# Attention behind a recurrent trunk: six PSUM banks for the projections, rotary tables in the first SwiGLU, rotation ahead of the norm

## The chip, the cores, the metric

The kernel is one program on one core of one Trainium2 chip. The metric is the device time of one execution, in microseconds (us), as the median of several executions. Its engines are TensorE (PE in the rows; PEld is its weight load), VectorE (DVE), ScalarE (ACT), GpSimd (POOL) and SyncE (SP). Each runs its own instructions in the order in which the program lists them and waits on the others through semaphores.

## The reference

A two-layer trunk over 512 tokens of 1024 features: a recurrent layer, a SwiGLU, then one attention layer with a shared K/V, and a second SwiGLU. The change lies in the attention, whose projections are normed per head and rotated:

```python
kv = (hn @ w_kv).reshape(B, S, N_GROUPS, 2, KV_HEADS, HEAD_DIM)   # 3 groups, 2 heads, 128
k = rms_norm(k, k_norm[:, None, :])
k = apply_partial_rope(k, cos, sin)      # first 32 of 128 features: x1*c - x2*s, x2*c + x1*s
...
q = (hn @ w_q)...                        # 3 groups x 2 kv heads x 4 query heads
q = rope(rms_norm(q, q_norm)); s = q @ k.T * HEAD_DIM ** -0.5
# softmax over a band: three dilation groups (windows 128, 512, 2048; dilations 1, 4, 16)
h = h + attention(...) @ w_o
h = h + (silu(h @ w_g) * (h @ w_u)) @ w_out
```

The norm is `y * rsqrt(mean(y*y) + eps) * gain`. Rows of the norm are single numbers per token and head, so the factor `rsqrt(...)` commutes with the rotation, which mixes features of one token and head only; the gain does not, since it differs from feature to feature.

## The kernel before, in words

The activations lie transposed, as eight tiles of 128 features x 512 tokens. Every fp32 product is made of three matmuls on high and low halves (`mm3`, L146 to L148; in the projections L676 to L678). Weights come through a class `Stream`: SP loads a 128x1024 piece (`wr`), ACT casts its high half (`wh`, L100), DVE subtracts the low one (`wl`, L107; for the query and output weights a DMA on POOL's queue adds it up). These steps have high priority; all else is ordered by a scheduler that works through the program once, so what stands in each engine's queue, and in which order, is fixed before the run.

PSUM has eight banks: four tagged "mm", two "PT" (transposes), one "S" (scores) and one "O" (values, row statistics). A tag's banks are handed out in turn, and a matmul that starts a new tile waits until all readers of the tile that had the bank before are done.

- **First SwiGLU** (`swiglu`, from L459). `norm_factors` sums squares (L240) and takes an inverse root on DVE (`rsqrt`, L205 to L215: eleven ops on 128x4, shift, subtract, and three Newton steps of three); DVE makes a diagonal `dg` (L252), a matmul spreads it over the rows (L255). Then per hidden block: `g` and `u` (L480, L482) on DVE, Silu on ACT, `u*g` on POOL (L483).
- **K/V projections** (`project`, L664). Three groups of four token tiles; each of four steps kk takes one weight piece and runs six matmuls on each of four tiles. A tile is ready after its fourth step and goes to `done_kv` (L699): `collect` copies the K half out of PSUM (L613, on ACT for K, on DVE for Q), squares it in place (L614) and sums it (L615); the V half is scaled and split by ACT (L713) and DVE (L714), in one piece per head for group 0, in two of 64 partitions per head for group 1. When the fourth tile is there, `normed` (L618) makes the inverse root (`factors`, L625 and `rsqrt`), then per tile `rotate`: one `scalar_tensor_tensor` per head for factor and gain (L635), and four ops of rotation (L642 to L645). `turn` transposes the result by PE (L730, L754). `at` and `tick` delay these calls by so many tile steps.
- **Rotary tables**. At the head of `attention`, ACT's queue issues four small loads (`far`, `grow`, `pos`, `inv`), and some 34 DVE ops on 128x128 (L542 to L582) with two Sin on ACT make `cc` and `ss`. They fall beside the first K/V projections.
- **Queries and attention**. The query projections of kv head 0 run like K/V. Those of kv head 1, and the first half of the output projection, are interleaved with attention units (`attend`, plan at the end of `attention`): per unit a `scores` call (nine matmuls into the bank S, L146 to L148; DVE's two fused reductions L804 and L807 into the negated maximum `mn`, Exp on ACT, L813, L814), three units later `turned` (transposes L829, split by ACT L223 into `ph` and DVE L224 into `pl`), and four units later `values`.

Of the kernel before, what the change touches and what calls it, by code (L numbers as in the profile page):

```python
# [139 lines left out]
def trunk(tc, A, out):  # L140
# [33 lines left out]
    with tc.tile_pool(name="keep", bufs=1) as kp, tc.tile_pool(name="wts", bufs=3) as wp, \  # L174
# [30 lines left out]
        def rsqrt(v, pool, tag):  # L205
            w = v.shape[-1]
            y = pool.tile([128, w], F32, name=tag + "y", tag=tag + "y")
            a = pool.tile([128, w], F32, name=tag + "a", tag=tag + "a")
            V.tensor_scalar(y.bitcast(I32), v.bitcast(I32), 1, None, ALU.arith_shift_right)
            V.tensor_scalar(y.bitcast(I32), y.bitcast(I32), -1.0, float(0x5F3759DF), ALU.mult, ALU.add)  # L210
            for _ in range(3):
                V.tensor_mul(a, y, v)
                V.scalar_tensor_tensor(a, a, -0.5, y, ALU.mult, ALU.mult)
                V.scalar_tensor_tensor(y, a, 1.5, y, ALU.add, ALU.mult)
            return y  # L215

# [17 lines left out]
        def gain(c, k):  # L234
            return par[:, c + k:c + k + 1]
# [250 lines left out]

        with tc.tile_pool(name="ffn1", bufs=2) as fp:
            fp = Pool(fp)

            def after_f1(m):  # L490
                split(h[m], gain(C_KV, m), xh[m], xl[m])
                squares(m, fp)

            swiglu(fp, p_f1, after_f1)


        with tc.tile_pool(name="att", bufs=2) as ap:
            ap = Pool(ap)
            attention(tc, A, ap, ws, dict(locals()))

# [15 lines left out]

def attention(tc, A, ap, ws, env):
    nc = tc.nc
    V, S, G, PE = nc.vector, nc.scalar, nc.gpsimd, nc.tensor
    h, xh, xl, ident, ssum = env["h"], env["xh"], env["xl"], env["ident"], env["ssum"]  # L520
    bank, mm3, split, halve, rsqrt = env["bank"], env["mm3"], env["split"], env["halve"], env["rsqrt"]
    gain, p_kv, p_q, p_o = env["gain"], env["p_kv"], env["p_q"], env["p_o"]

    far = ap.tile([128, 4, 160], BF16, name="far", bufs=1)
    S.dma_start(far, A["far"])
    grow = ap.tile([128, 6, 128], F32, name="grow", bufs=1)
# [4 lines left out]
    pos = ap.tile([128, 8], I32, name="pos", bufs=1)  # L531
    S.dma_start(pos, A["pos"])
    inv = ap.tile([128, 16], F32, name="inv", bufs=1)
    S.dma_start(inv, A["inv_freq"])
    posf = ap.tile([128, 8], F32, name="posf", bufs=1)
    V.tensor_copy(posf, pos)
    cc = ap.tile([128, 8, 16], F32, name="cc", bufs=1)
    ss = ap.tile([128, 8, 2, 16], F32, name="ss", bufs=1)

    tmp = [ap.tile([128, 512], F32, name="rtmp", tag="pr", bufs=N_PR) for _ in range(2)]  # L540
    ang, a1, a0, s1, k2, t = (tmp[i % 2][:, 128 * (i // 2):128 * (i // 2) + 128] for i in range(6))
# [75 lines left out]

    def normed(st, nh, tab, g_row, E, turn, lag, tiles=range(4)):  # L618
# [11 lines left out]
        def rotate(t):  # L630
            dst, r = kn[t], st["r"]
# [5 lines left out]
            x = dst.rearrange("q (h d) -> q h d", d=128)[:, :nh]  # L637
            a = ap.tile([128, 4, 32], F32, name="ra", tag="ra")[:, :nh]
            b = ap.tile([128, 4, 32], F32, name="rbt", tag="rbt", bufs=1)[:, :nh]
            cct = cc[:, tab + t].unsqueeze(1).unsqueeze(1).to_broadcast([128, nh, 2, 16])  # L640
            sst = [ss[:, tab + t, c, :].unsqueeze(1).to_broadcast([128, nh, 16]) for c in range(2)]
            E.tensor_tensor(*(v.rearrange("q h (c f) -> q h c f", c=2) for v in (a, x[:, :, 0:32])), cct, ALU.mult)  # L642
            E.tensor_tensor(b[:, :, 0:16], x[:, :, 16:32], sst[0], ALU.mult)
            E.tensor_tensor(b[:, :, 16:32], x[:, :, 0:16], sst[1], ALU.mult)
            E.tensor_tensor(x[:, :, 0:32], a, b, ALU.add)  # L645

        at(1, factors)
        for j, t in enumerate(tiles):
            at(2 + j, lambda t=t: rotate(t))
            at(lag + j, lambda t=t: turn(t, kn[t]))  # L650
# [47 lines left out]
    for g in range(3):  # L698
        def done_kv(t, ps, g=g, st={}):  # L699
            tab = 0 if g == 0 else 4  # L700
            c = slice(128 * t, 128 * t + 128)
            vv = ps[:, 256:512].rearrange("q (a d) -> q a d", a=2)
            collect(ps, 2, t, 4, st, S.copy)
            ro = rstd[0][:, tab + t:tab + t + 1]
# [20 lines left out]
            if t == 3:  # L725
# [18 lines left out]
    def project_q(kv):  # L744
        for g in range(3):

            for j, tiles in enumerate((range(2), range(2, 4)) if kv and g == 2 else (range(4),)):
                def done_q(t, ps, g=g, st={}, tiles=tiles):
                    collect(ps, 4, t - tiles[0], len(tiles), st, V.tensor_copy)
                    if t == tiles[-1]:  # L750
# [32 lines left out]
    def scores(kv, n, p):  # L783
# [39 lines left out]
    def turned(kv, n, p):  # L823
# [174 lines left out]
```

## Time and profile before

| | us |
|---|---|
| median of 3 executions | 1232.18 (1232.13 to 1233.57) |
| the profiled execution | 1235.38 |
| its span in the trace | 1233.6 |
| PE busy / DVE / ACT / POOL | 1212.2 / 686.5 / 514.8 / 113.7 |

The profile is of one execution. Its own time stands 1.8 us above the span (what lies before and after) and 3.2 us above the median. PE is busy 98% of the span, so what can be won lies in the 21.4 us in which it is not, and in stretches in which its granted clock is not full. A row of the timeline gives the start, the duration, the engine, the line, and in brackets how long the engine stood idle before it and on which instruction it waited.

### The profile page before, as it was taken

Reading aid. Unit: us, or ns where it says so; the run is one execution under the profiler, and the core shown is the slowest. Engines: PE = TensorE matmul, PEld = TensorE weight load, DVE = VectorE, ACT = ScalarE, POOL = GpSimd, SP = SyncE. Lnnn points to the kernel's source line nnn. Section 1 sums busy time; section 2 is a strip of 40 time slices with the busy share of each in tenths; the row PEclk is TensorE's granted clock in tenths of the full one; section 3 lists DMA queues with packets and bytes.
Section 4 is the critical chain, followed back from the end, with each engine's and each line's share of the span. In section 5 each row is a group of like instructions: output and inputs, shape, how many; then the busy total and the mean of one; then the engine's idle time right before and its main releaser. Section 6 shows DMA issues by size and latency. Waiting matters only on the chain.

```text
span 1233.6 us, 14762 instructions
## 1 busy us (share of the span) xinstructions
PE 1212.2 (98%) x5629; PEld 998.7 (81%) x5629; DVE 686.5 (56%) x1382; ACT 514.8 (42%) x771; POOL 113.7 (9%) x128
## 2 busy tenths in 40 slices
PE   9999999999999999998999999899999999999998
PEld 6778888888888888877888888798888888888887
DVE  7877654455454333387567677875645545443221
ACT  5795432323222222265555666665423323222110
POOL 0100001011111000010411010000001111100000
PEclk9999999999999999999999998999999999999999
DMA  6544323323323333332988665435232232333331
GB/s 224 141 116 120 103 86 103 103 88 100 99 89 99 97 104 98 102 96 85 210 183 186 137 143 132 103 69 120 86 103 88 101 96 92 103 99 103 117 116 45
DMA packets 40902, 138.15 MB, mean 112 GB/s; under 512 B 5120, under 2 KB 5760, under 8 KB 40832
## 3 DMA queue, kind: packets, MB, share of 16 engines
q1 hardware_dynamic: 32688, 111.74, 28.6%
q0 software_dynamic: 6848, 24.12, 11.4%
q10 hardware_dynamic: 1296, 1.36, 0.4%
q8 instruction: 44, 0.72, 0.2%
q14 instruction: 26, 0.21, 0.1%
HBM read 134.05 MB, written 2.10 MB: 110 GB/s over the span
## 4 chain that ended last, share of the span: by engine, by line
PE 92%; DVE 3%; ACT 3%; DMA 1%; issue 0%; ACTq 0%
PE ps L147 25%; PE ps L146 25%; PE ps L148 25%; PE ps L676 4%; PE ps L677 4%; PE ps L678 4%; PE ps L754 1%; ACT wh L100 1%; PE ps L829 1%; PE ps L382 1%; DVE kn L635 1%; DMA wr<-in_w_in 1%; PE ps L383 0%; ACT qh L223 0%; ACT wl L103 0%
## 5 line engine op out<-in xcount | busy, mean ns | idle before, releaser
L100 ACT CAST wh<-wr 128x1024 fp32r<-128x1024 f32 (+3 forms) x212 | 215.4, 1016 | 499.9 <-PE ps L147 448.4
L146 PE MATMUL ps<-xh,wh 128*128 128x512 f32 x896 | 355.2, 397 | 1.2 <-ACT xh L218 1.2
L147 PE MATMUL ps<-xl,wh 128*128 128x512 f32 x896 | 349.5, 390 | 0.3 <-DVE xl L219 0.3
L148 PE MATMUL ps<-xh,wl 128*128 128x512 f32 x896 | 349.8, 390 | 0.0
L107 DVE TENSOR_TENSOR wl<-wr,wh 128x1024 fp32r<-128x1024 f32 (+2 forms) x168 | 241.5, 1438 | 153.8 <-ACT wh L100 153.7
L146 PEld LDWEIGHTS ps<-xh,wh 128*128 128x128 f32 x896 | 168.7, 188 | 39.4 <-ACT xh L218 2.6
L147 PEld LDWEIGHTS ps<-xl,wh 128*128 128x128 f32 x896 | 168.6, 188 | 37.7 <-issue 2.6
L148 PEld LDWEIGHTS ps<-xh,wl 128*128 128x128 f32 x896 | 168.5, 188 | 35.4 <-DMA wl<-in_w_in 0.2
L146 PE MATMUL ps<-gh,wh 128*128 128x512 f32 x352 | 136.9, 389 | 0.0
L147 PE MATMUL ps<-gl,wh 128*128 128x512 f32 x352 | 136.9, 389 | 0.0
L148 PE MATMUL ps<-gh,wl 128*128 128x512 f32 x352 | 136.9, 389 | 0.0
L482 DVE TENSOR_TENSOR u<-ps,rb 128x512 f32<-128x512 f32 x44 | 30.4, 691 | 139.2 <-PE ps L148 139.2
L483 POOL TENSOR_TENSOR u<-u,g 128x512 f32<-128x512 f32 x44 | 58.0, 1318 | 497.9 <-ACT wh L100 364.5
L676 PE MATMUL ps<-wh,xh 128*128 128x512 f32 x224 | 92.1, 411 | 0.1
L678 PE MATMUL ps<-wh,xl 128*128 128x512 f32 x224 | 88.6, 395 | 0.0
L677 PE MATMUL ps<-wl,xh 128*128 128x512 f32 x224 | 88.4, 395 | 0.0
L148 PEld LDWEIGHTS ps<-gh,wl 128*128 128x128 f32 x352 | 66.1, 188 | 13.8
L146 PEld LDWEIGHTS ps<-gh,wh 128*128 128x128 f32 x352 | 66.1, 188 | 13.7
L147 PEld LDWEIGHTS ps<-gl,wh 128*128 128x128 f32 x352 | 66.1, 188 | 13.6
L480 DVE TENSOR_TENSOR g<-ps,rb 128x512 f32<-128x512 f32 x44 | 30.4, 691 | 64.5 <-PE ps L148 64.4
L103 ACT ACTIVATE wl<-wr 128x1024 fp32r<-128x1024 f32 x44 | 46.6, 1058 | 26.6 <-PE ps L677 25.6
L223 ACT CAST gh<-u 128x512 fp32r<-128x512 f32 x44 | 27.3, 621 | 59.9 <-POOL u L483 59.9
(202 smaller groups left out, 1457.4 us busy)
## 6 DMA issues: line engine op xcount, KB each, us to landing
wr<-in_f_in SPq DMA_DIRECT2D x88, 512.0 KB, 3.5
wr<-in_f_out SPq DMA_DIRECT2D x32, 512.0 KB, 3.6
wr<-in_w_q SPq DMA_DIRECT2D x28, 512.0 KB, 6.6
wl<-in_w_q POOLq DMA_DIRECT2D x28, 512.0 KB, 7.1
wr<-in_w_in SPq DMA_DIRECT2D x14, 512.0 KB, 3.9
wr<-in_f_out SPq DMA_DIRECT2D x16, 384.0 KB, 3.1
wr<-in_w_kv SPq DMA_DIRECT2D x12, 512.0 KB, 3.4
wl<-in_w_in POOLq DMA_DIRECT2D x8, 512.0 KB, 6.5
```

The costliest lines, as they stand in the source:

```text
L100: nc.scalar.copy(hi[:, c], r[:, c])
L103: nc.scalar.mul(lo[:, c], r[:, c], -1.0)
L107: a = eng.tensor_tensor(lo[:, c], r[:, c], hi[:, c].bitcast(F32), ALU.subtract)
L146: PE.matmul(ps, wh, xh, start=first, stop=False)
L147: PE.matmul(ps, wh, xl, start=False, stop=False)
L148: PE.matmul(ps, wl, xh, start=False, stop=last)
L480: V.tensor_tensor(g, pair[0], rb, ALU.mult)
L482: V.tensor_tensor(u, pair[1], rb, ALU.mult)
L483: G.tensor_tensor(u, u, g, ALU.mult)
L676: PE.matmul(ps[t], xh[k][:, r], wh[:, c], start=k == 0, stop=False)
L677: PE.matmul(ps[t], xh[k][:, r], wl[:, c], start=False, stop=False)
L678: PE.matmul(ps[t], xl[k][:, r], wh[:, c], start=False, stop=k == 7)
```

## The change

Six edits, all around the attention:

1. `project` takes its banks from a list: four "mm", then "S", then "O", four times over, which covers the 12 K/V tiles and the 12 query tiles of kv head 0; after that "mm" alone.
2. The loads and the ops of the rotary tables move out of `attention` into a function `rotary`, called in the first SwiGLU's program at its first output block, with the tables in a pool of their own.
3. `collect` multiplies by the gain while it takes the tile out of PSUM, on DVE for K and Q alike (ACT's copy of K goes).
4. The rotation is done per tile one step after `collect`, before the norm's factor is known; the factor is then one `tensor_tensor` per tile (`scale`) with a broadcast factor.
5. `rsqrt` has eight ops in place of eleven: one op for the start value, one Newton step of three and one step of higher order of four.
6. The softmax of a score and the split of its transposed rows get high priority in the scheduler.

```diff
-            V.tensor_scalar(y.bitcast(I32), v.bitcast(I32), 1, None, ALU.arith_shift_right)
-            V.tensor_scalar(y.bitcast(I32), y.bitcast(I32), -1.0, float(0x5F3759DF), ALU.mult, ALU.add)
-            for _ in range(3):
-                V.tensor_mul(a, y, v)
-                V.scalar_tensor_tensor(a, a, -0.5, y, ALU.mult, ALU.mult)
-                V.scalar_tensor_tensor(y, a, 1.5, y, ALU.add, ALU.mult)
+            V.tensor_scalar(y.bitcast(I32), v.bitcast(I32), -0.5, float(0x5F3759DF), ALU.mult, ALU.add)
+
+            s = 0.375
+            V.tensor_mul(a, y, v)
+            V.scalar_tensor_tensor(a, a, -0.5 * s, y, ALU.mult, ALU.mult)
+            V.scalar_tensor_tensor(y, a, 1.5 * s, y, ALU.add, ALU.mult)
+            V.scalar_tensor_tensor(a, y, -1.0 / (s * s), v, ALU.mult, ALU.mult)
+            V.tensor_mul(a, a, y)
+            V.scalar_tensor_tensor(a, a, 10.0 / 3.0, a, ALU.add, ALU.mult)
+            V.scalar_tensor_tensor(y, a, 5.0, y, ALU.add, ALU.mult)
...
+                def after_f1(m):
+                    split(h[m], gain(C_KV, m), xh[m], xl[m])
+                    squares(m, fp)
+                    if m == 0:
+                        tables.extend(rotary(tc, A, rp, fp))
...
-    def collect(raw, nh, j, n, st, copy):
+    def collect(raw, nh, j, n, st, tab, g_row):
...
-        copy(dst[:, :128 * nh], rows)
+        x = dst.rearrange("q (h d) -> q h d", d=128)[:, :nh]
+        V.tensor_tensor(x, rows.rearrange("q (h d) -> q h d", d=128),
+                        grow[:, g_row].unsqueeze(1).to_broadcast([128, nh, 128]), ALU.mult)
...
+        at(1, lambda: rotate(x, nh, tab))
...
-            for i in range(nh):
-                c = slice(128 * i, 128 * i + 128)
-                j = nh * (t - first) + i
-                V.scalar_tensor_tensor(dst[:, c], dst[:, c], r[:, j:j + 1], grow[:, g_row, :],
-                                       ALU.mult, ALU.mult)
...
+        def scale(t):
+            j = nh * (t - first)
+            x = kn[t].rearrange("q (h d) -> q h d", d=128)[:, :nh]
+            V.tensor_tensor(x, x, st["r"][:, j:j + nh].unsqueeze(2).to_broadcast([128, nh, 128]), ALU.mult)
...
+    free = itertools.chain(["mm", "mm", "mm", "mm", "S", "O"] * 4, itertools.repeat("mm"))
...
-                    ps[t] = bank()
+                    ps[t] = bank(next(free))
...
+    @first
+    def softmax(n, p, ps, pr, mn, g0, w, nb):
...
-        halve(pt.rearrange("q (b k) -> q b k", k=128)[:, :nb], ph[:, :nb, p % 2], pl[:, :nb, p % 2])
+        first(halve)(pt.rearrange("q (b k) -> q b k", k=128)[:, :nb], ph[:, :nb, p % 2], pl[:, :nb, p % 2])
```

How this moves instructions, at three places on DVE. In the rows a name stands for a tile (buffer numbers left in where they tell pieces apart); the lines of the changed kernel are its own.

DVE at the front of the first SwiGLU, where `nrv` to `nry` are the inverse root for the row factors and `dg` its diagonal, before:

```order
L214 SCALAR_TENSOR_TENSOR nry<-nra,nry 128x4
L212 TENSOR_TENSOR nra<-nry,nrv 128x4
L213 SCALAR_TENSOR_TENSOR nra<-nra,nry 128x4
L214 SCALAR_TENSOR_TENSOR nry<-nra,nry 128x4
L252 TENSOR_SCALAR dg<-ident,nry 128x128 x4
L107 TENSOR_TENSOR wl_1479<-wr_1445,wh_1478 128x1024
L480 TENSOR_TENSOR g<-ps,rb 128x512
```

and in the changed kernel:

```order
L217 SCALAR_TENSOR_TENSOR nra<-nra 128x4
L536 TENSOR_SCALAR grow<-grow 128x384
L218 SCALAR_TENSOR_TENSOR nry<-nra,nry 128x4
L544 CAST posf<-pos 128x8
L256 TENSOR_SCALAR dg<-ident,nry 128x128 x4
L550 TENSOR_TENSOR rtmp<-posf,inv 128x128
L555 TENSOR_SCALAR rtmp<-rtmp 128x128
```

The scheduler brought the tables' ops from the first output block to the very front: the op on `grow`, which waits for a load, now stands ahead of the last step of the inverse root and of `dg`; ten rows of the tables (some grouping several ops) follow before the next `wl`, and the rest stands behind it, up to the second `u`.

DVE in the K/V projections, where the first tiles of group 0 come out of PSUM, before (`rtmp`, `cc`, `ss` are the tables):

```order
L615 TENSOR_REDUCE sqc<-ps 128x2
L574 SCALAR_TENSOR_TENSOR rtmp<-rtmp 128x128
L714 SCALAR_TENSOR_TENSOR vl_3708<-ps,msy,vh_3706 128x128
L575 TENSOR_SCALAR rtmp<-rtmp 128x128
L714 SCALAR_TENSOR_TENSOR vl_3708<-ps,msy,vh_3706 128x128
L579 TENSOR_TENSOR rtmp<-rtmp 128x128
L578 TENSOR_TENSOR rtmp<-rtmp 128x128
L582 TENSOR_SCALAR cc<-rtmp 128x128
L581 TENSOR_SCALAR ss<-rtmp 128x8x16 x2
L714 SCALAR_TENSOR_TENSOR vl_3709<-ps,msy,vh_3707 128x128 x2
```

and in the changed kernel:

```order
L633 TENSOR_TENSOR kn<-ps,grow 128x256
L737 SCALAR_TENSOR_TENSOR vl_3707<-ps,msy,vh_3705 128x128
L648 TENSOR_TENSOR kn<-ra,rbt 128x2x32
L645 TENSOR_TENSOR ra<-kn,cc 128x64
L636 TENSOR_REDUCE sqc<-ps 128x2
L737 SCALAR_TENSOR_TENSOR vl_3708<-ps,msy,vh_3706 128x128
L646 TENSOR_TENSOR rbt<-kn,ss 128x2x16
L647 TENSOR_TENSOR rbt<-kn,ss 128x2x16
```

The tables are gone from between the V pieces; the gain's product and the rotation of the tile before stand there instead.

DVE in the attention stage, where the last two-tile block of queries of kv head 1 is normed, before (`qr4y` is the factor, `pl` and `pr` belong to attention units):

```order
L213 SCALAR_TENSOR_TENSOR qr4a<-qr4a,qr4y 128x8
L214 SCALAR_TENSOR_TENSOR qr4y<-qr4a,qr4y 128x8
L635 SCALAR_TENSOR_TENSOR kn<-kn,qr4y,grow 128x128 x5
L642 TENSOR_TENSOR ra<-kn,cc 128x128
L643 TENSOR_TENSOR rbt<-kn,ss 128x4x16
L644 TENSOR_TENSOR rbt<-kn,ss 128x4x16
L635 SCALAR_TENSOR_TENSOR kn<-kn,qr4y,grow 128x128
L645 TENSOR_TENSOR kn<-ra,rbt 128x4x32
L635 SCALAR_TENSOR_TENSOR kn<-kn,qr4y,grow 128x128 x2
```

and in the changed kernel:

```order
L217 SCALAR_TENSOR_TENSOR qr4a<-qr4a 128x8
L218 SCALAR_TENSOR_TENSOR qr4y<-qr4a,qr4y 128x8
L665 TENSOR_TENSOR kn<-kn,qr4y 128x512
L228 TENSOR_TENSOR pl<-ps,ph 128x4x128
L665 TENSOR_TENSOR kn<-kn,qr4y 128x512
L842 ISA pr,mn<-ps,ssum 128x256
L842 ISA mn 128x1
L845 ISA pr,mn<-ps,far,mn 128x256
```

From the factor to the first tile that can be transposed stood five scalings, three ops of rotation, a sixth scaling and the rotation's sum; now one `scale`. The two reductions of a softmax (L842, L845) stand side by side, where three ops of rotation stood between them before.

## Rows read from the trace of the kernel before

**Rows 1.** The page: busy time of each engine over the span.

```profile
PE 1212.2 (98%) x5629; PEld 998.7 (81%) x5629; DVE 686.5 (56%) x1382; ACT 514.8 (42%) x771; POOL 113.7 (9%) x128
```

**Rows 2.** Windows by stage: start and end, length, then busy time and (instructions) of PE, PEld, DVE, ACT and POOL, the granted clock as a share, the DMA share, GB/s. 525 to 602 holds the K/V projections, 602 to 698 the queries of kv head 0, 698 to 802 attention beside the queries of kv head 1.

```profile
525.00:545.00 20.00, 18.00 (x88) 14.88 (x87) 17.39 (x62) 14.69 (x32) 2.95 (x4) 1.00 0.36 110
...
570.00:602.00 32.00, 31.75 (x135) 25.67 (x136) 19.73 (x84) 17.15 (x37) 8.87 (x14) 0.95 0.55 134
602.00:698.00 96.00, 96.00 (x470) 79.77 (x469) 61.02 (x226) 53.98 (x81) 17.43 (x22) 1.00 0.83 180
698.00:720.00 22.00, 21.53 (x129) 18.19 (x128) 14.60 (x62) 12.42 (x23) 2.19 (x3) 1.00 0.52 120
720.00:802.00 82.00, 74.17 (x461) 64.45 (x460) 67.55 (x245) 55.20 (x105) 8.20 (x10) 0.94 0.56 129
```

**Rows 3.** PE's waits over the whole span: the line that waited, for what, total us, times, longest.

```profile
PE ps L676 <- DVE vl L714: 5.2, 2, 3.2
PE ps L146 <- DVE mn L807: 3.5, 4, 1.9
PE ps L146 <- ACT ph L223: 2.1, 2, 1.7
PE ps L754 <- DVE kn L645: 2.1, 2, 1.6
```

**Rows 4.** Timeline of PE in the K/V projections: matmuls before, and after, a wait.

```profile
543.91 0.47 PE L676 MATMUL ps<-wh,xp 128*128 128x512 f32 x1 [2.00 <-DVE vl L714]
...
549.00 0.39 PE L676 MATMUL ps<-wh,xp 128*128 128x512 f32 x1
549.22 0.39 PE L677 MATMUL ps<-wl,xp 128*128 128x512 f32 x1
...
570.16 0.47 PE L676 MATMUL ps<-wh,xp 128*128 128x512 f32 x1 [3.21 <-DVE vl L714]
570.46 0.58 PE L677 MATMUL ps<-wl,xp 128*128 128x512 f32 x1
...
573.83 0.46 PE L676 MATMUL ps<-wh,xp 128*128 128x512 f32 x1
```

**Rows 5.** Timeline of DVE and ACT in the K/V projections, where the first tiles of groups 0 and 1 come out of PSUM.

```profile
543.14 0.36 DVE L581 TENSOR_SCALAR ss<-rtmp 128x128 f32<-128x128 f32 x2
543.42 0.60 DVE L714 SCALAR_TENSOR_TENSOR vl<-ps,msy,vh 128x128 fp32r<-128x128 f32 x2
...
562.89 0.37 ACT L613 COPY kn<-ps 128x256 f32<-128x256 f32 x1 [0.39 <-PE ps L678]
...
568.40 1.23 DVE L107 TENSOR_TENSOR wl<-wr,wh 128x1024 fp32r<-128x1024 f32 x1 [0.52 <-ACT wh L100]
...
569.66 1.00 DVE L714 SCALAR_TENSOR_TENSOR vl<-ps,msy,vh 64x128 fp32r<-64x128 f32 x3
```

**Rows 6.** Timeline of DVE in the attention stage: a softmax's reductions among rotation ops, and a norm's scaling and rotation.

```profile
738.36 0.42 DVE L804 CUSTOM_DVE_ANT_0 pr<-ps,ssum 128x256 f32<-128x256 f32 x1
738.70 0.29 DVE L642 TENSOR_TENSOR ra<-kn,cc 128x128 f32<-128x128 f32 x1
739.18 0.48 DVE L807 CUSTOM_DVE_ANT_1 pr<-ps,far,mn 128x256 f32<-128x256 f32 x1
...
757.99 0.17 DVE L214 SCALAR_TENSOR_TENSOR qr4y<-qr4a,qr4y 128x8 f32<-128x8 f32 x1
758.19 1.40 DVE L635 SCALAR_TENSOR_TENSOR kn<-kn,qr4y,grow 128x128 f32<-128x128 f32 x5
...
760.25 0.28 DVE L645 TENSOR_TENSOR kn<-ra,rbt 128x128 f32<-128x128 f32 x1
```

**Rows 7.** DVE's groups of instructions between 698 and 802 us: count, busy time and mean ns of one, idle time ahead of them and its releaser.

```profile
L635 DVE SCALAR_TENSOR_TENSOR kn<-kn,qr4y,grow 128x128 f32<-128x128 f32 x48 | 14.2, 346 | 0.1
L804 DVE CUSTOM_DVE_ANT_0 pr<-ps,ssum 128x256 f32<-128x256 f32 (+1 forms) x20 | 7.7, 384 | 1.5 <-PE ps L148 1.3
L613 DVE COPY kn<-ps 128x512 f32<-128x512 f32 x8 | 5.5, 683 | 3.4 <-PE ps L678 3.4
```

**Rows 8.** The page's groups over the span: a product out of PSUM on DVE (columns as in rows 7).

```profile
L482 DVE TENSOR_TENSOR u<-ps,rb 128x512 f32<-128x512 f32 x44 | 30.4, 691 | 139.2 <-PE ps L148 139.2
```

**Rows 9.** Timeline of DVE, PE and POOL at the front of the first SwiGLU.

```profile
160.16 0.69 DVE L232 TENSOR_TENSOR ssum<-ssum,sq 128x512 f32<-128x512 f32 x1
...
167.08 0.88 DVE L252 TENSOR_SCALAR dg<-ident,nry 128x128 f32<-128x128 f32 x4
...
169.08 1.02 PE L255 MATMUL ps<-dg,ones 128*128 128x512 f32 x2
...
176.48 1.22 DVE L107 TENSOR_TENSOR wl<-wr,wh 128x1024 fp32r<-128x1024 f32 x1 [0.17 <-ACT wh L100]
...
181.06 0.69 DVE L482 TENSOR_TENSOR u<-ps,rb 128x512 f32<-128x512 f32 x1 [3.35 <-PE ps L148]
181.90 1.29 POOL L483 TENSOR_TENSOR u<-u,g 128x512 f32<-128x512 f32 x1 [7.68 <-DVE u L482]
181.96 2.30 DVE L107 TENSOR_TENSOR wl<-wr,wh 128x1024 fp32r<-128x1024 f32 x1 [0.21 <-ACT wh L100]
```

**Rows 10.** DVE's groups of instructions between 525 and 545 us (columns as in rows 7): the commonest op of the rotary tables.

```profile
L551 DVE SCALAR_TENSOR_TENSOR rtmp<-rtmp 128x128 f32<-128x128 f32 x13 | 3.7, 287 | 0.1
```

**Rows 11.** DMA issues between 518 and 540 us: what is loaded, the queue, KB, us from issue to landing.

```profile
grow<-in_row_gains ACTq DMA_DIRECT2D x1, 384.0 KB, 6.5
```

More of the change, by code (lines that the diff above doesn't have):

```diff
@@ L485, in swiglu @@
             out_proj(p[1], HB, 8, gh, gl, after)
[L487 to L499, printed above, removed]
+        with tc.tile_pool(name="tables", bufs=1) as rp:
+            rp = Pool(rp)
+            with tc.tile_pool(name="ffn1", bufs=2) as fp:
+                fp = Pool(fp)
+                tables = []
+                def after_f1(m):
[3 more added lines that the diff above has]
+                        tables.extend(rotary(tc, A, rp, fp))
+                swiglu(fp, p_f1, after_f1)
+            with tc.tile_pool(name="att", bufs=2) as ap:
+                ap = Pool(ap)
+                attention(tc, A, ap, ws, dict(locals()))
         with tc.tile_pool(name="ffn2", bufs=2) as fp:
@@ L514, with rotary @@
 START_Q = 11
-def attention(tc, A, ap, ws, env):
+def rotary(tc, A, rp, tp):
     nc = tc.nc
[L519 to L524, printed above, removed]
+    V, S = nc.vector, nc.scalar
+    rp.tile([128, 16], F32, name="pad")
+    far = rp.tile([128, 4, 160], BF16, name="far", bufs=1)
     S.dma_start(far, A["far"])
-    grow = ap.tile([128, 6, 128], F32, name="grow", bufs=1)
+    grow = rp.tile([128, 6, 128], F32, name="grow", bufs=1)
     S.dma_start(grow, A["row_gains"])
     V.tensor_scalar(grow[:, 3:6], grow[:, 3:6], -(128.0 ** -0.5), None, ALU.mult)
-    pos = ap.tile([128, 8], I32, name="pos", bufs=1)
+    pos = rp.tile([128, 8], I32, name="pos", bufs=1)
     S.dma_start(pos, A["pos"])
-    inv = ap.tile([128, 16], F32, name="inv", bufs=1)
+    inv = rp.tile([128, 16], F32, name="inv", bufs=1)
     S.dma_start(inv, A["inv_freq"])
-    posf = ap.tile([128, 8], F32, name="posf", bufs=1)
+    posf = rp.tile([128, 8], F32, name="posf", bufs=1)
     V.tensor_copy(posf, pos)
-    cc = ap.tile([128, 8, 16], F32, name="cc", bufs=1)
-    ss = ap.tile([128, 8, 2, 16], F32, name="ss", bufs=1)
-    tmp = [ap.tile([128, 512], F32, name="rtmp", tag="pr", bufs=N_PR) for _ in range(2)]
+    cc = rp.tile([128, 8, 16], F32, name="cc", bufs=1)
+    ss = rp.tile([128, 8, 2, 16], F32, name="ss", bufs=1)
+    tmp = [tp.tile([128, 512], F32, name="rtmp") for _ in range(2)]
     ang, a1, a0, s1, k2, t = (tmp[i % 2][:, 128 * (i // 2):128 * (i // 2) + 128] for i in range(6))
@@ L582, in attention @@
     V.tensor_scalar(cc, a1.rearrange("q (c f) -> q c f", f=16), -2.0, 1.0, ALU.mult, ALU.add)
+    return far, grow, cc, ss
+def attention(tc, A, ap, ws, env):
+    nc = tc.nc
+    V, S, G, PE = nc.vector, nc.scalar, nc.gpsimd, nc.tensor
+    h, xh, xl, ident, ssum = env["h"], env["xh"], env["xl"], env["ident"], env["ssum"]
+    bank, mm3, split, halve, rsqrt = env["bank"], env["mm3"], env["split"], env["halve"], env["rsqrt"]
+    gain, p_kv, p_q, p_o = env["gain"], env["p_kv"], env["p_q"], env["p_o"]
+    far, grow, cc, ss = env["tables"]
+    ap.tile([128, 112], F32, name="pad", bufs=1)
     def by_phase(t):
@@ L616, in collect, with rotate, normed @@
         st["kn"].append(dst)
-    def normed(st, nh, tab, g_row, E, turn, lag, tiles=range(4)):
+        at(1, lambda: rotate(x, nh, tab))
+    def rotate(x, nh, tab):
+        a = ap.tile([128, 4, 32], F32, name="ra", tag="ra")[:, :nh]
+        b = ap.tile([128, 4, 32], F32, name="rbt", tag="rbt", bufs=1)[:, :nh]
+        cct = cc[:, tab].unsqueeze(1).unsqueeze(1).to_broadcast([128, nh, 2, 16])
+        sst = [ss[:, tab, c, :].unsqueeze(1).to_broadcast([128, nh, 16]) for c in range(2)]
+        V.tensor_tensor(*(v.rearrange("q h (c f) -> q h c f", c=2) for v in (a, x[:, :, 0:32])), cct, ALU.mult)
+        V.tensor_tensor(b[:, :, 0:16], x[:, :, 16:32], sst[0], ALU.mult)
+        V.tensor_tensor(b[:, :, 16:32], x[:, :, 0:16], sst[1], ALU.mult)
+        V.tensor_tensor(x[:, :, 0:32], a, b, ALU.add)
+    def normed(st, nh, tab, turn, lag, tiles=range(4)):
         kn = dict(zip(tiles, st["kn"]))
@@ L628, in factors @@
             st["r"] = rsqrt(sq.rearrange("q t i -> q (t i)"), ap, f"qr{nh}")
-        def rotate(t):
-            dst, r = kn[t], st["r"]
-            for i in range(nh):
-                c = slice(128 * i, 128 * i + 128)
-                j = nh * (t - first) + i
-                V.scalar_tensor_tensor(dst[:, c], dst[:, c], r[:, j:j + 1], grow[:, g_row, :],
-                                       ALU.mult, ALU.mult)
[L637 to L645, printed above, removed]
+        def scale(t):
+            j = nh * (t - first)
+            x = kn[t].rearrange("q (h d) -> q h d", d=128)[:, :nh]
+            V.tensor_tensor(x, x, st["r"][:, j:j + nh].unsqueeze(2).to_broadcast([128, nh, 128]), ALU.mult)
         at(1, factors)
         for j, t in enumerate(tiles):
-            at(2 + j, lambda t=t: rotate(t))
+            at(2 + j, lambda t=t: scale(t))
             at(lag + j, lambda t=t: turn(t, kn[t]))
@@ L702, in done_kv @@
             vv = ps[:, 256:512].rearrange("q (a d) -> q a d", a=2)
-            collect(ps, 2, t, 4, st, S.copy)
+            collect(ps, 2, t, 4, st, tab + t, g)
             ro = rstd[0][:, tab + t:tab + t + 1]
@@ L732, in turn @@
                         halve(pt[:, 128 * a:128 * a + 128], kh[a][g][:, c], kl[a][g][:, c])
-                normed(st, 2, tab, g, V, turn, 10)
+                normed(st, 2, tab, turn, 10)
         for _ in project(p_kv + 4 * g, *((xh, xl) if g == 0 else (xph, xpl)), done_kv):
@@ L748, in done_q @@
                 def done_q(t, ps, g=g, st={}, tiles=tiles):
-                    collect(ps, 4, t - tiles[0], len(tiles), st, V.tensor_copy)
+                    collect(ps, 4, t - tiles[0], len(tiles), st, t, 3 + g)
                     if t == tiles[-1]:
@@ L759, in turn, with first, run @@
                                 query_part(0, 0, g)
-                        normed(st, 4, 0, 3 + g, V, turn, 8 if len(tiles) > 2 else 5, tiles)
+                        normed(st, 4, 0, turn, 8 if len(tiles) > 2 else 5, tiles)
                 yield from project(p_q + 12 * kv + 4 * g + 4 * j, xh, xl, done_q, tiles)
+    def first(fn):
+        def run(*args):
+            with tc.high_priority():
+                return fn(*args)
+        return run
     o_t = ap.tile([128, 4, 384], F32, name="o_t", bufs=1)
@@ L803, in scores @@
         mn = ap.tile([128, 2], F32, name="mn", bufs=4)
+        softmax(n, p, ps, pr, mn, g0, w, nb)
+        prs[kv, n, p] = pr
+        if n < 3 and p == (2 if kv else 3) or not kv and p == 3 and (0, 1, 2) in qt:
+            query_parts(kv + n // 3, (n + 1) % 4)
+    @first
+    def softmax(n, p, ps, pr, mn, g0, w, nb):
+        width = g0 + 2 * w
         V.tensor_tensor_reduce(pr[:, :g0], ps[:, :g0], near[:, p, 256 - g0:256], 1.0, 3e38,
@@ L814, in scores @@
         V.tensor_scalar(pr[:, :width], pr[:, :width], den, None, ALU.mult)
-        prs[kv, n, p] = pr
-        if n < 3 and p == (2 if kv else 3) or not kv and p == 3 and (0, 1, 2) in qt:
-            query_parts(kv + n // 3, (n + 1) % 4)
     def blocks(n, p):
```

## The prediction

> **What bounds the kernel now.** I read the page's busy times first: PE works 1212.2 of 1233.6 us [rows 1], so a change off PE is worth only what it gives back of PE's idle time, plus what a reduced clock costs. Then the windows, to see where PE is not full. In the queries of kv head 0 it is (96.00 of 96.00); the gaps lie in two stages, the K/V projections from 525 to 602 and attention from 698 to 802 [rows 2]. Then PE's waits, which name what was late: DVE's low half of V (5.2 us in two waits), the running minimum `mn` of a softmax (3.5 in four), the split of transposed softmax rows (2.1 in two), a rotated query tile `kn` (2.1 in two) [rows 3]. That is 12.9 us, and all four are what this change touches.
>
> The clock takes more. After the wait of 3.21 us the matmuls from 570.46 to 573.83, eight of them, stand 0.42 us apart, where full clock has 0.22 [rows 4]: half clock, 1.2 in place of 2.4 GHz, for 3.4 us, which costs 8 x 0.20 = 1.6 us. The window agrees: 5% of 32 us is 1.6. In attention the granted clock is 0.94 over 82 us [rows 2], so 4.9 us, three such stretches. A stall of 2.00 us at 543.91 drew none [rows 4]. Together 12.9 + 1.6 + 4.9 = 19.4 us can be won, 6.8 of it (5.2 + 1.6) in K/V and 12.6 (7.7 + 4.9) in attention.
>
> **The change, part by part.**
>
> *Banks.* With four banks, tile 5 of a stream waits until tile 1 is out of PSUM; the time for that is three tile steps of six matmuls, about 4.1 us (3 x 6 x 0.227). With six banks it is two steps of 1.37 us more, 6.85. In K/V the first wait was 2.00 us and ended at 543.91, so the bank was needed at 541.91 and will be needed at 544.65, after it came free before: the wait goes (2.0 us). The second: group 1's first tile is copied at 562.89, its bank was needed at 570.16 - 3.21 = 566.95, and was free 7.3 us after the copy began. The need moves to 569.7, so with unchanged evacuation 0.5 us would be left. It is not unchanged: K's copy moves from ACT (0.37 [rows 5]) to DVE, and each tile's rotation, about 0.6 us by the order's four small ops at the spacing of [rows 6], stands among the V pieces; a `wl` of 1.23 us stands there before and after [rows 5]. Against that, ACT is freer. Summing DVE's rows in the new order at these prices, the first tile's bank comes free 6.7 to 7.2 us after its end and the second one's up to 10, where 8.2 is allowed. I take 1.3 us for what is left, wait and some half clock, the middle between nothing and 2.6. **K/V gives 5.5 us; ends 2.0 (only the first wait goes) and 6.8.**
>
> *Rotary tables away from K/V.* The last table op stands just ahead of the V pieces that freed the first bank (543.14, then 543.42 [rows 5]), so their leaving helps that same wait. With the later need it was gone anyway; I count nothing twice.
>
> *Rotary tables in the SwiGLU.* They are some 34 ops; thirteen took 3.7 us [rows 10], the others are alike, so 8 to 9 us on DVE, plus four loads on ACT's queue. Two things there can reach PE. First, DVE's op on `grow` waits for a load that took 6.5 us [rows 11], and `dg` is queued behind it. The tables' space becomes free no earlier than the last sum of squares at 160.85 [rows 9]; one DMA issue later the load lands at about 167.8, `grow` and the last step of the inverse root follow, and `dg` (0.88) is ready at about 169.3. PE takes it at 169.08 and was not idle there: 0.2 us late, or nothing. Second, ten rows of tables stand ahead of one `wl`, and more ahead of the next, which ran at 176.48. DVE has slack there (3.35 us idle before 181.06 alone), and PE takes that `wl` in the block that follows 181.0 [rows 9]; I get it done at about 180.8. **Cost 0.5 us; ends 0 and 4** (a wait of 2.4 that also draws a half-clock stretch of 1.6).
>
> What speaks against this place is in [rows 9] too: the same subtraction `wl` takes 1.22 us alone and 2.30 when it begins 0.06 us after POOL's product, 1.08 more. The Trainium skill's page "SBUF — State Buffer", section "Who interferes with whom", says why: a DVE instruction with two SBUF inputs contends with a GpSimd one that reads SBUF, and the second to issue fully blocks; the tables are full of such ops. By that rule the trace agrees, and two POOL products in the stretch would hold DVE by up to 1.3 us each; that is inside the ends above and a rival below.
>
> *Gain at the evacuation, rotation before the norm, one scaling per tile.* For Q the copy becomes a product from PSUM, 0.683 against 0.691 us [rows 7, 8]: nothing. Four scalings per tile become one op over 512 elements. 48 scalings took 14.2 us of DVE's time between 698 and 802 [rows 7]; twelve products at 0.69 take 8.3. On the path to a transpose stood, after the factor, five scalings (1.40), the rotation's ops and its sum, from 758.19 to 760.53 [rows 6], 2.3 us; now one scaling of 0.69. With the shorter root (three ops fewer at 0.2 us spacing [rows 6], 0.6) the tile is ready 2.2 us earlier, more than the 1.6 that PE waited for it. Both `kn` waits should go with the half clock behind the long one: 2.1 + 1.6 = 3.7; I take 3.4.
>
> *Softmax first.* Three rotation ops stood between the two reductions of a softmax (738.36 to 739.66 [rows 6]), and whole blocks of scaling ahead. In the new order they stand side by side with one small op at most between. But PE's order now also puts a score earlier, and the bank "S" is one bank: a score still waits for the reductions of the last. Of 3.5 us and a half-clock stretch of 1.6 I take half, 2.6. The split into `ph` is ACT's, where the order of its instructions stays; of its 2.1 + 1.6 I take 1.6. **Attention gives 3.4 + 2.6 + 1.6 = 7.6; ends 3 and 12.6.**
>
> *Where the root is shorter elsewhere* (row factors, token statistics) it stands beside PE's work with over 1 us to spare (`dg` done at 167.96, taken at 169.08 [rows 9]): nothing.
>
> **Sum:** 5.5 + 7.6 - 0.5 = 12.6 us. The profiled execution of 1235.4 would come to 1222.8; it lies 3.2 over the median, so I forecast 1232.2 - 12.6 = **1219.6**.
>
> **The rivals.**
>
> *A. All waits go.* For it: DVE has 82.2 us of work in the 104 us of attention [rows 2] and loses 7.4 of it (5.9 in scalings, nine small ops). Against it: one bank for scores, and ACT's order unchanged. 1232.2 - 19.4 = 1212.8. Chance 0.12.
>
> *B. The scores' bank takes attention's gain.* PE reaches the next score sooner and waits for `mn` there; each wait long enough draws half clock. Attention gives 2 only: 5.5 + 2 - 0.5 = 7.0, 1225.2. Chance 0.21.
>
> *C. The SwiGLU's front pays 4 us*, by the late load or by DVE held beside POOL: 5.5 + 7.6 - 4 = 9.1, 1223.1. Chance 0.08.
>
> *D. Slower: the softmax blocks DVE's queue.* With priority its reductions stand ahead of ready work, and DVE, in order, stands idle at each until PE has made the score, while the evacuation of a projection tile is queued behind, in a stage that is back at four banks. Before, DVE idled 1.5 us ahead of 20 such reductions, 0.08 each [rows 7], which speaks against it. DVE will have 74.8 us of work in 104, so 29 us to lose: it decides from 1.5 us per score. At 2.0 DVE needs 114.8, the stage is 10.8 longer, and with K/V's 5.5 and the front's 0.5 the sum is 5.8 slower: 1238.0. Chance 0.10.
>
> *E. It does not do what it says.* DVE's added work per K tile puts the V pieces as late as before, so six banks only save the first wait, and attention's waits change their names: 2.0 - 0.5, 1230.7. Chance 0.09.
>
> **How the numbers follow.** The forecast has 0.40; its own range, by the ends of the terms, is 1214 to 1225. A measurement here tells 0.2% apart, 2.5 us, so E counts as the same. Faster is the forecast with A, B and C, 0.81; same 0.09; slower 0.10. The range 1212.5 to 1228.5 holds all but D and E.
>
> **What would show it.** In the trace after: no wait for `vl` at group 1's first tile, at most 2 us at the next group's; no wait for `kn`; waits for `mn` and `ph` of some 3 us together with at most two half-clock stretches, so a granted clock near 0.97 from 720 to 802; in the first SwiGLU under 1 us before the `dg` matmul, and none at the second hidden block. A `wl` of over 2 us among the tables would show C's contention. I am wrong if PE's idle time in the two stages stays over 9 us, if `mn` waits grow in number, or if a wait of over 2 us opens before 185 us.

## The result, and the profile after

The changed kernel takes **1221.70 us**, median of 4 executions (1220.86 to 1223.05); the kernel before, run beside it, 1232.88 of 4 (1232.13 to 1233.92). The ratio is 0.9906 with a 95% interval of 0.9892 to 0.9919: 10 to 13 us faster. 1219.6 was forecast, 12.6 us faster. The profiled execution took 1221.2 us, its span is 1219.4. One execution of all that follow, in E4, took 1336.25 us at a granted clock of 0.85 and is left out of its median.

The spans differ by 14.2 us, more than the medians, because the profiled execution of before was itself a long one. Part of that lies ahead of the first SwiGLU: the last sum of squares there, at 160.16 before [rows 9], now begins at 158.92. Of this the shorter root gives about 0.4 us (see E7); the rest differs between executions, since E1 and E11, which change nothing up to there, have it at 159.20 and 161.35. So the stages are compared by PE's idle time and clock, not by their start times.

The page's busy times after, to hold against [rows 1]:

```profile
PE 1206.4 (99%) x5629; PEld 995.0 (82%) x5629; DVE 671.0 (55%) x1268; ACT 512.2 (42%) x759; POOL 113.4 (9%) x128
```

The windows after, columns as in [rows 2]:

```profile
525.00:545.00 20.00, 20.00 (x91) 16.63 (x92) 16.17 (x48) 12.24 (x23) 0.71 (x2) 1.00 0.33 100
545.00:570.00 25.00, 25.00 (x113) 20.07 (x113) 19.76 (x63) 12.21 (x30) 0.00 (x0) 1.00 0.30 99
570.00:602.00 32.00, 32.00 (x148) 26.25 (x147) 19.43 (x77) 18.80 (x36) 14.16 (x21) 1.00 0.75 177
698.00:720.00 22.00, 21.95 (x134) 19.04 (x133) 12.38 (x42) 13.66 (x25) 2.36 (x3) 1.00 0.44 97
720.00:802.00 82.00, 76.45 (x511) 67.56 (x510) 66.56 (x227) 57.42 (x117) 8.03 (x10) 0.98 0.58 129
```

and PE's waits in attention, as in [rows 3]:

```profile
PE ps L146 <- ACT ph L227: 1.5, 1, 1.5
PE ps L146 <- DVE mn L845: 1.5, 2, 1.0
...
PE ps L777 <- DVE kn L665: 0.9, 1, 0.9
...
PE ps L777 <- ACT qt L779: 0.8, 1, 0.8
PE ps L146 <- ACT qh L227: 0.6, 1, 0.6
```

K/V shows no wait and full clock: its 5.2 us and the 1.6 of half clock are back, 6.8. Attention's idle time from 698 to 802 fell from 8.3 to 5.6 us, and its clock loss from 4.9 (0.94 of 82) to 1.6 (0.98): 6.0. PE's busy time fell by 5.8 us with the same 5629 matmuls: 4.9 of it is the clock in these windows (1.6 in K/V, 3.3 in attention).

The clock part holds for this pair of executions only. The kernel before was granted 0.994 to 0.997 over its span in the 39 executions that were run beside E1 to E12, 0.9956 on average, and the profiled one, at 0.994, is at the low end; the changed kernel had 0.997 to 0.999. One part in a thousand is 1.2 us, so some 2 us of what the two traces differ by are not the change.

### The profile page after: what moved, and what is told of

Same layout as the page of the kernel before. It is cut to its first block, busy times and chain, and to the rows that moved or that the text cites. A ratio compares the mean times of both kernels' runs of the same rounds, so it can differ in the third digit from the quotient of the medians.

```text
span 1219.4 us, 14615 instructions
## 1 busy us (share of the span) xinstructions
PE 1206.4 (99%) x5629; PEld 995.0 (82%) x5629; DVE 671.0 (55%) x1268; ACT 512.2 (42%) x759; POOL 113.4 (9%) x128
## 4 chain that ended last, share of the span: by engine, by line
PE 92%; DVE 4%; ACT 3%; DMA 1%; issue 0%; ACTq 0%
PE ps L148 25%; PE ps L147 25%; PE ps L146 24%; PE ps L699 5%; PE ps L701 5%; PE ps L700 5%; PE ps L777 1%; ACT wh L100 1%; PE ps L864 1%; DMA wl<-in_w_in 1%; PE ps L386 1%; PE ps L387 0%; DMA wr<-in_w_in 0%; ACT wl L103 0%; PE ps L244 0%
```

## The experiments

Each is given against before, in the medians and ratios of its own runs. "E" numbers follow the labels.

**E1, six banks alone.** The kernel before with

```diff
+    free = itertools.chain(["mm", "mm", "mm", "mm", "S", "O"] * 4, itertools.repeat("mm"))
-                    ps[t] = bank()
+                    ps[t] = bank(next(free))
```

> The kernel before with the six banks alone. Theory (the banks are what K/V waited for): both waits of the K/V projections (5.2 us) and the half-clock stretch behind the second (1.6) go, attention keeps its 12.6 us: 6 to 7 us faster than before, about 1226. Rival (DVE's table ops and V pieces are what is late, the banks only move the wait): the first wait goes, 1.5 us or more stays at the second, perhaps with its half-clock stretch: 2 to 4 us faster, about 1229.

1227.97 us, ratio 0.9959 (0.9946 to 0.9971): 5.1 us faster. Of K/V's two waits one of half a microsecond is left, at the second group, and no half clock:

```profile
525.00:602.00 77.00, 76.51 (x350) 62.73 (x350) 59.56 (x229) 47.73 (x105) 16.19 (x24) 1.00 0.50 131
720.00:802.00 82.00, 73.29 (x482) 63.60 (x482) 67.95 (x256) 56.96 (x113) 8.66 (x10) 0.98 0.54 121
```

K/V gave 6.3 us in this trace. The theory holds; the rival's 1.5 us or more is not there. Attention kept its waits (`mn` 3.4 us in four, `ph` 2.2, `kn` 2.1), but not its 12.6 us: the same waits drew a clock of 0.98 here (1.6 us) and of 0.94 in the trace of before (4.9 us).

**E2, the changed kernel with four banks** (`ps[t] = bank()` put back).

> The changed kernel with four banks for the projections. Theory: K/V's waits come back, and since K's evacuation and the rotation now stand on DVE among the V pieces they come back at least as long: 5 to 8 us slower than the changed kernel, 1227 to 1230. Rival (moving the tables off was what freed K/V): under 2 us slower, below 1224.

1228.44, ratio 0.9963 (0.995 to 0.9975): 6.7 us slower than the changed kernel (7.0 by the ratios), as the theory had it. One K/V wait is back, not two:

```profile
PE ps L699 <- DVE vl L737: 3.2, 1, 3.2
```

The window of K/V has 73.68 us of PE in 77 at a clock of 0.98, so 3.3 + 1.5 us of the difference; of the rest, 1.6 is a lower clock in attention (0.96 against 0.98). The first wait stays away without the banks: the tables that stood there have left.

**E11, the tables' move alone** (the diff's `rotary` and its pool on the kernel before).

> The kernel before with the rotary tables moved alone. Theory (tables and banks each remove the first wait of K/V, only the banks the second): the 2.0 us wait goes, the 3.2 us wait with its half-clock stretch stays: 1 to 2.5 us faster than before. Rival (the tables hide either way): no change, or slower by a wait at the front of the first SwiGLU.

1232.74, ratio 0.9991 (0.9982 to 1.0), 1.1 us: the interval ends at no change. The trace agrees with the theory on the waits: of K/V's two only one is left. It does not agree on the clock: no half clock follows the wait, and the matmuls behind it stand 0.22 to 0.23 us apart at once.

```profile
PE ps L692 <- DVE vl L730: 3.2, 1, 3.2
...
569.33 0.47 PE L692 MATMUL ps<-wh,xp 128*128 128x512 f32 x1 [3.21 <-DVE vl L730]
569.64 0.39 PE L693 MATMUL ps<-wl,xp 128*128 128x512 f32 x1
569.86 0.39 PE L694 MATMUL ps<-wh,xp 128*128 128x512 f32 x1
```

**E3, the changed kernel with the tables back in attention** (the call in `after_f1` taken out, `rotary(tc, A, ap, ap)` at the head of `attention`).

> The changed kernel with the rotary tables made at the head of attention again. Theory (with six banks the tables hide either way): within 1.5 us of the changed kernel, 1220 to 1223, no wait over 0.5 us in K/V. Rival (the tables delay the V pieces beyond even the later need): one or two waits of 1 to 2 us in K/V, 1224 or more.

1223.09, ratio 0.9921 (0.9908 to 0.9935), against 0.9906 for the changed kernel: the intervals overlap. PE has 76.89 of 77 us in K/V and waits for nothing on DVE there. With six banks the tables hide at either place, so edits 1 and 2 both remove the first wait, and only the banks the second.

**E6, the norm's edits alone** (gain at the evacuation, rotation ahead, one scaling, shorter root; four banks, tables in attention, no priority).

> The kernel before with the norm's edits alone (gain at the evacuation, rotation ahead, one scaling, shorter root): four banks, tables at the head of attention, no priority. Theory (attention's gain is theirs): K/V keeps its two waits (5 us) and the half-clock stretch, longer by what K's evacuation on DVE adds, attention gains 4 to 6: 3 to 6 us faster than before, 1226.5 to 1229.5. Rival (attention's gain came with banks or tables, which start it earlier): within 2 us of before.

1233.08 of 11 executions, ratio 0.9998 (0.9986 to 1.001): nothing, where 3 to 6 us were expected; the rival has the time right, but not the cause. Attention did gain: 4.9 us idle from 698 to 802 against 8.3, and the waits for `mn` and `ph` are down without banks, tables or priority:

```profile
PE ps L146 <- DVE mn L840: 1.6, 3, 0.7
...
PE ps L146 <- ACT ph L227: 1.4, 1, 1.4
```

With the clock (0.96 from 720 to 802) this is 5.0 us by the traces. K/V took 2.7 of it back. PE's rows at the first wait:

```profile
545.60 0.50 PE L695 MATMUL ps<-wh,xp 128*128 128x512 f32 x1 [3.05 <-DVE vl L733]
...
546.67 0.63 PE L695 MATMUL ps<-wh,xp 128*128 128x512 f32 x1
547.09 0.63 PE L696 MATMUL ps<-wl,xp 128*128 128x512 f32 x1
```

The first wait grew from 2.00 to 3.05 us, and half clock followed it, which it did not in [rows 4]; the second kept its 3.2. The window of K/V has 70.55 us of PE at a clock of 0.96. Two waits of 1.46 and 0.21 us for a low half of the query weights came on top; whether these belong to the edits is not shown. K's product and the rotation on DVE stay hidden only where the banks give DVE the time. The tables' leaving helps in part: E2, which differs from E6 by their move and the priority, is 4.3 us faster by the ratios.

**E4 and E5, the changed kernel without priority for softmax and split.**

```diff
-            with tc.high_priority():
-                return fn(*args)
+            return fn(*args)
```

> The changed kernel without the priority for softmax and split. Theory (priority takes scores' reductions out of the queue behind norm work): waits for the running minimum come back to 3 to 5 us with one or two half-clock stretches: 3 to 5 us slower than the changed kernel, 1225 to 1227. Rival (the lighter norm work alone freed DVE, priority only packs the scores): within 1 us of it.

> The changed kernel without the priority for softmax and split, once more, for a trace at full clock: its median was 1222.1, that of the changed kernel 1221.7. Theory as it stands now (the lighter norm freed DVE, priority only renames waits): PE's idle time from 698 to 802 within 1.5 us of the changed kernel's 5.6, the waits under other names. Rival (priority gains some us in attention, and the median hides it): idle time of 8 us or more, with a half-clock stretch more.

1222.08, ratio 0.9909 (0.9894 to 0.9924), and 1222.06, ratio 0.9911 (0.9898 to 0.9925): the changed kernel's time. E5's attention:

```profile
698.00:802.00 104.00, 99.45 (x654) 86.71 (x652) 78.60 (x270) 71.87 (x143) 10.36 (x12) 1.00 0.56 126
```

Less idle time (4.6 us against 5.6) and full clock. The `mn` waits have the same total as with priority:

```profile
PE ps L146 <- DVE mn L844: 1.5, 3, 0.7
```

The rival of E4 holds: the lighter norm freed DVE, as E6 shows by itself, and the priority adds nothing that the medians tell.

**E7, the changed kernel with the old root.**

> The changed kernel with the old root of eleven ops. Theory (three ops of 0.2 us stand on the path to the one transpose that PE still waits for, 0.95 us): that wait grows by 0.6, to 1.5, and may draw a half-clock stretch: 0.6 to 2.2 us slower than the changed kernel. Rival (the root hides everywhere): no change, within 0.5 us, the wait as long as before.

1224.28, ratio 0.9927 (0.9915 to 0.994), about 2.6 us slower than the changed kernel by ratios, with intervals that just touch. The wait in attention grew by 0.6, as expected, and a new one of 0.6 us stands in K/V, where keys are transposed. In the recurrent layer PE waits 0.9 us for `rate`, as in before, E1 and E11, which have the old root too; every trace with the new root has 0.4 or 0.5. E7's waits, and the changed kernel's for `rate`:

```profile
PE ps L773 <- DVE kn L661: 1.6, 1, 1.6
...
PE ps L382 <- ACT rate L389: 0.9, 1, 0.9
...
PE ps L749 <- DVE kn L661: 0.6, 1, 0.6
```

```profile
PE ps L386 <- ACT rate L393: 0.5, 1, 0.5
```

These are 1.6 us; no further half clock shows, so the rest of the difference stays within the spread.

**E8, the values' split at priority too** (`first(halve)(src[:, i], ...)`).

> The changed kernel with the split of the attention's values at high priority too, to get ACT to the transposed rows sooner: ACT stood 1.43 us behind DVE's low half of the values there, and PE then 1.54 us for them, with half clock after. Theory: that wait and its half-clock stretch shrink or go, up to 3 us faster than the changed kernel, about 1219 to 1221. Rival (the low half stays behind the inverse root's ops in DVE's queue): the wait stays, no change.

1221.24, ratio 0.9911 (0.9896 to 0.9927): no change; PE's wait for `ph` is 1.54 us as before. The rival holds: priority moved other pieces, while the first subtraction stayed behind the root's ops.

**E9 and E10, copies grouped**, with and without priority:

```diff
-            for i in range(4):
-                halve(src[:, i], his[i], los[i])
+            for i in range(4):
+                S.copy(his[i], src[:, i])
+            for i in range(4):
+                V.tensor_tensor(los[i], src[:, i], his[i].bitcast(F32), ALU.subtract)
```

> The changed kernel with the split of the attention's values regrouped: ACT's four copies out of the bank first, then DVE's four subtractions, so ACT is not held once per piece by DVE. Theory (ACT's wait of 1.43 us for DVE's first subtraction, queued behind an inverse root, is what made the transposed rows late): PE's wait of 1.54 us for them falls below 0.5 and the half-clock stretch of 1.7 goes: 2.5 to 3 us faster than the changed kernel, about 1219. Rival (ACT is simply full there): the wait stays over 1 us.

> The same regrouping without the priority for softmax and split, which had 4.6 us idle in attention against 5.5. Theory: the wait of 1.38 us for the transposed rows shrinks to below 0.5, some 3 us of short waits are left, no half-clock stretch: 1218.5 to 1220.5, the best of all kernels if the difference is to be told. Rival: ACT's four copies in a row now stand ahead of the transposed rows, and the wait stays.

> The changed kernel once more, on one chip with the three others, as the base of their differences: 1220 to 1223, the same waits.

On one chip: changed kernel (E12) 1223.13, ratio 0.9914 (0.9898 to 0.9929); E9 1221.66, 0.9901 (0.9887 to 0.9914); E10 **1219.06**, 0.9882 (0.9869 to 0.9896). The grouping did what it said: ACT's rows in E10 show four copies in a row and no wait for DVE,

```profile
772.99 0.77 ACT L897 CAST xh<-ps 128x128 fp32r<-128x128 f32 x4 [0.51 <-PE ps L148]
...
774.93 0.41 ACT L227 CAST ph<-ps 128x256 fp32r<-128x256 f32 x1
```

but PE then waited for the other half of the same pair, E9's row and E10's:

```profile
778.70 0.39 PE L147 MATMUL ps<-pl,vh 128*128 128x256 f32 x1 [1.46 <-DVE pl L228]
```

```profile
778.11 0.38 PE L147 MATMUL ps<-pl,vh 128*128 128x256 f32 x1 [1.11 <-DVE pl L228]
```

So the theory of E9 fell: DVE's queue, not ACT's wait, sets when the pair is there, since `pl` stands behind the root and a scaling on DVE, in E9:

```profile
776.53 0.17 DVE L218 SCALAR_TENSOR_TENSOR qr4y<-qr4a,qr4y 128x8 f32<-128x8 f32 x1
...
776.95 0.68 DVE L665 TENSOR_TENSOR kn<-kn,qr4y 128x512 f32<-128x512 f32 x1
...
778.23 0.42 DVE L228 TENSOR_TENSOR pl<-ps,ph 128x256 fp32r<-128x256 f32 x1
```

E10 beats the changed kernel by some 3 to 4 us in that comparison; its trace has no half clock from 698 to 802 and 4.5 us idle, where E12 has 0.96 over the 82 us, 3.3 us:

```profile
698.00:802.00 104.00, 99.54 (x655) 86.69 (x654) 80.42 (x275) 72.75 (x146) 10.37 (x12) 1.00 0.56 122
```

```profile
720.00:802.00 82.00, 76.50 (x500) 67.77 (x499) 65.86 (x224) 57.55 (x116) 8.48 (x10) 0.96 0.58 127
```

Most of that is the clock: E12 was granted 0.997 over the span in all four executions, E9 0.999, E10 0.999 or 1.0, and the 0.002 to 0.003 between E12 and E10 are 2.5 to 3.7 us. How much of it is the priority left out, how much the grouping and how much only those executions isn't settled: E5, without the grouping, has the same idle time and clock, but its median was no better than the changed kernel's.

## Why the prediction was right

**Banks: 5.5 forecast, 6.8 measured** by the traces, 5.1 by E1's median. The mechanism was right: E1 has it with no other edit, with the 0.5 us left that the text worked out for an unchanged evacuation. The evacuation in the new order was priced right too, and what was mis-sized is the allowance. DVE's rows at group 1's first tiles after the change, then PE's weight loads that waited for the two banks, and PE's matmuls:

```profile
560.21 0.41 DVE L633 TENSOR_TENSOR kn<-ps,grow 128x256 f32<-128x256 f32 x1
...
565.00 1.22 DVE L107 TENSOR_TENSOR wl<-wr,wh 128x1024 fp32r<-128x1024 f32 x1
566.24 0.73 DVE L737 SCALAR_TENSOR_TENSOR vl<-ps,msy,vh 64x128 fp32r<-64x128 f32 x2
...
568.56 0.36 DVE L737 SCALAR_TENSOR_TENSOR vl<-ps,msy,vh 64x128 fp32r<-64x128 f32 x1
```

```profile
566.66 0.19 PEld L699 LDWEIGHTS ps<-wh,xp 128*128 128x128 f32 x1 [0.22 <-DVE vl L737]
568.97 0.19 PEld L699 LDWEIGHTS ps<-wh,xp 128*128 128x128 f32 x1 [0.40 <-DVE vl L737]
```

```profile
558.96 0.39 PE L701 MATMUL ps<-wh,xp 128*128 128x512 f32 x1
...
566.01 0.39 PE L699 MATMUL ps<-wh,xp 128*128 128x512 f32 x1
566.24 0.39 PE L700 MATMUL ps<-wl,xp 128*128 128x512 f32 x1
566.47 0.39 PE L701 MATMUL ps<-wh,xp 128*128 128x512 f32 x1
566.69 0.46 PE L699 MATMUL ps<-wh,xp 128*128 128x512 f32 x1
```

The first tile's last matmul begins at 558.96. Its bank is free when the first of the two pieces at 566.24 is done (0.36, like the piece at 568.56), at 566.60, 7.2 us after the tile's end (6.7 to 7.2 forecast); the second's at 568.92, 9.6 us after that same end (up to 10 forecast). But PE needs the first bank only at 566.69, 7.3 us after the end and not 6.85: 33 matmuls stand between, five steps of six and three more, which already use the next weight piece (the one of `wl` begins at 566.24, when the `wl` of 565.00 is done). Three more stand ahead of the second. So PE loses nothing at the first bank and 0.13 us at the second, by the spacing of its matmuls, and the 1.3 us set aside came to almost nothing. The sum took PE's order as fixed steps; the scheduler had put ready matmuls into the gap. E2 and E11 bear out that the tables' leaving removes the same first wait as the banks and must not be added.

**Tables in the SwiGLU: 0.5 forecast, 0 measured.** PE is busy 20.00 of 20 us from 160 to 180. The front after, DVE and PE:

```profile
164.93 0.35 DVE L536 TENSOR_SCALAR grow<-grow 128x384 f32<-128x384 f32 x1
...
165.39 0.88 DVE L256 TENSOR_SCALAR dg<-ident,nry 128x128 f32<-128x128 f32 x4
...
167.85 1.02 PE L259 MATMUL ps<-dg,ones 128*128 128x512 f32 x2
```

`dg` is done at 166.27, 1.6 us ahead of PE. Two prices were off: the load landed 4.5 us after its issue at 160.36, not 6.5 as in [rows 11], and the root is shorter by three ops. The contention is there, as [rows 9] had it: three ops of the tables took 1.91 us beside POOL's product (172.20 to 173.55), and 0.94 without it,

```profile
167.75 0.94 DVE L559 SCALAR_TENSOR_TENSOR rtmp<-rtmp 128x128 f32<-128x128 f32 x3
...
171.79 1.91 DVE L559 SCALAR_TENSOR_TENSOR rtmp<-rtmp 128x128 f32<-128x128 f32 x3
...
172.20 1.35 POOL L487 TENSOR_TENSOR u<-u,g 128x512 f32<-128x512 f32 x1 [70.99 <-DVE rtmp L559]
```

and DVE's slack took it. The Trainium skill's page "SBUF — State Buffer", section "Who interferes with whom", says that a DVE instruction with two SBUF inputs contends with a GpSimd instruction that reads SBUF. This trace agrees: 0.97 us for one product.

**Attention: 7.6 forecast, 6.0 measured**, 2.7 of it idle time and 3.3 clock, with its parts dealt out wrongly. `kn` (3.4 forecast): the short wait is gone and the long one shrank from 1.6 to 0.95 us, where the text had the tile ready before PE comes; no half clock follows it, so 2.1 + 1.6 - 0.95 = 2.8. `mn` (2.6): 3.5 + 1.6 fell to 1.5, 3.6. `ph` (1.6): 2.1 + 1.6 became 1.5 + 1.6, 0.6. New waits for `qt` and `qh` (1.4 against 0.5 before) took 0.9 back. The 1.6 credited to `kn` and `mn` each is a stretch of half clock that E1, with the same waits as before, did not have either; the waits alone fell by 1.2, 2.0 and 0.6. The clause that failed is "softmax first": it was credited with the gain on `mn` and `ph`, 4.2 us, and E4 and E5 show the same time and no more idle without it. Nor do the two reductions always stand together, as the text had it; a product of 0.69 us can stand between them:

```profile
771.36 0.29 DVE L842 CUSTOM_DVE_ANT_0 pr<-ps,ssum 128x128 f32<-128x128 f32 x1
...
771.67 0.69 DVE L633 TENSOR_TENSOR kn<-ps,grow 128x512 f32<-128x512 f32 x1
772.28 0.34 DVE L845 CUSTOM_DVE_ANT_1 pr<-ps,far,mn 128x128 f32<-128x128 f32 x1
```

What freed `mn` are the norm's edits, since E6, with these alone, has 1.6 us of it. The reading behind it, that the scalings and rotations which stood among the reductions [rows 6] are fewer and earlier, is argued: gain, rotation and scaling were not run apart. The rivals B and D did not come: `mn` waits fell from four to two, and DVE stood idle 2.3 us ahead of 22 first reductions, 0.1 each, where D needed 1.5.

**The root "elsewhere: nothing"** missed K's transposes, where E7 shows 0.6 us for three ops, and the wait for `rate`, 0.4.

**What the sum did not say.** It added terms as if each edit brought its own. E6 shows that they do not: the norm's edits alone bring nothing, since K/V and the query weights lose at four banks most of what they win in attention. The total held because the change has the banks too, and in part by luck: the 4.2 us credited to the priority came from the norm's edits, the 1.3 us kept back for K/V was not needed, and attention gave less. 6.8 + 6.0 = 12.8 by the traces stands against 11.2 by the medians (10.0 to 13.3); the forecast read half clock off an execution that had more of it than most and took its price off the median.

**The range.** The ends of the terms, added up, are 1 and 19.4 us, 1231.2 to 1212.8, and not the 1214 to 1225 that the text draws from them; the measured time lies in both. Of the signs named, those for K/V, for the clock (0.98), for `mn` and `ph` together (3.0 us) and for the first SwiGLU came; the one for `kn` did not.

## What to carry to other kernels

When a producer waits for its output banks, count the time from a tile's end to its bank's next use and compare it with the evacuation's length: two more banks moved the need by some 2.7 us here (two tile steps of six matmuls at 0.227) and by themselves left 0.5 of 5.2 us of waits. Take the need from PE's order as the scheduler leaves it, not from the loop: three matmuls that it had put ahead made up for a late evacuation here. Work that is moved onto the evacuating engine has to be priced together with that allowance; the same edits gave nothing at four banks with the tables beside them. A priority that puts one consumer first should be tested alone: here it only exchanged waits, and the version without it was at least as fast.

## What the runs showed of the hardware

The half clock after a wait doesn't follow from the wait's length alone. Waits of 2.00 us (before) drew none, 3.05 us (E6) and 1.54 us (after) did, and 1.38 us (E5) none. At one and the same wait, 3.20 us in E2 drew a stretch and 3.21 us in E11 drew none; in attention the waits of 1.90, 1.62 and 1.70 us of before each drew one, and of the 1.88, 1.61 and 1.70 us of E1 only the last did. A single trace therefore does not price a wait's half clock. With the same list of waits, the changed kernel's granted clock from 720 to 802 us was 0.98 in one execution and 0.96 in another (E12), some 1.6 us of difference between executions. The four small loads took 3.5 to 4.5 us to land at the front of the SwiGLU (after), 5.2 to 6.5 beside the K/V projections (before).
